# A decoder step on one core: the norms' scales spread by transposes of whole tiles instead of products with the identity

## The chip, the cores and the metric

The kernel runs on one NeuronCore of a Trainium2 chip. Its engines work side by side, each through its own queue in order: TensorE (PE in the profile, its weight loads PEld) multiplies matrices, VectorE (DVE) and ScalarE (ACT) work elementwise, GpSimd (POOL) does small things and issues the DMAs that add into memory, SyncE (SP) issues the other loads and stores. TensorE writes to PSUM, from which DVE and ACT read. The metric is the device time of one execution in microseconds, as the median of several runs; less is better.

## What is computed

One inference step of a small two-layer decoder in float32: 512 new prompt tokens and 8 sequences of 4 new sample tokens, 544 tokens in all, of width 1024. Layer 0 mixes with a short gated convolution, layer 1 with multi-scale retention (4 heads, a state of 256 x 512 for each sequence and head); each is followed by a gated feed-forward block of width 2816.

```python
def rmsnorm(x, g):
    xf = x.astype(jnp.float32)
    y = xf * lax.rsqrt(jnp.mean(xf * xf, axis=-1, keepdims=True) + RMS_EPS)
    return (y * g.astype(jnp.float32)).astype(x.dtype)

def swiglu(x, w_gate, w_up, w_down):
    return (jax.nn.silu(x @ w_gate) * (x @ w_up)) @ w_down

def trunk(x, ...):
    for i in range(DEPTH):
        h = rmsnorm(x, norm_mix[i])
        m, st = short_conv_mixer(h, ...) if i % 2 == 0 else retention_mixer(h, ...)
        x = x + m
        x = x + swiglu(rmsnorm(x, norm_ffn[i]), ffn_w_gate[i], ffn_w_up[i], ffn_w_down[i])
    return rmsnorm(x, final_norm), ...
```

There are thus five norms: the convolution's, the first feed-forward block's, the retention's, the second feed-forward block's and the final one. What the change touches is the per-token factor of each, 1 / sqrt(mean of x squared + eps).

## The kernel before

The activations stand transposed: eight tiles `x[k]` of 128 features (partitions) by 544 tokens (columns), in two halves of HT = 272 tokens. Prompt and sample tokens go through the same matrix products. Each float32 operand is split into a high and a low part (`split`, `split_x`), and a product is three matmuls of 272 columns on these parts (`project`, line 187; `product`, line 386, which does the blocks of a scheme of seven products for two by two). Weights come by SP's queue; for some, the low part is made by ACT writing the negated high part and POOL's queue adding the weights on top with a DMA (`split_adding`, `mixed`, lines 211 and 318).

A norm's gain is applied when the activations are split; its per-token factor is multiplied in only later, behind the products, so that the products need not wait for it. The factor is made by the generator `rms_scale`, whose steps are woven between the matmuls of other products:

1. The squares are summed over the eight tiles into `sqacc` (`square_sum`).
2. Five or six matmuls with one moving column (line 272) take the mean over the 128 partitions, for one tile of 128 tokens each; the result stands as a column of one value per token, in PSUM. Tile 4 is the last 128 tokens (416 to 543), so it overlaps tile 3.
3. `rsqrt` adds eps on DVE and takes the power on POOL, into `rN`, 128 partitions by up to 6 columns.
4. After `rest` more steps of the weave, the scales are spread over all partitions: `spread` (line 252) multiplies the column `rN[:, tt]`, repeated 128 times by a zero step as the stationary operand, with columns of the identity matrix `ident` as the moving operand. Each partition of the output then holds the scales of that tile's tokens along the columns. The tokens are cut where the halves meet: products of 128, 128 and 16 columns fill half 0 (272), of 112, 128 and 32 columns half 1.
5. ACT copies both halves from PSUM into `R` (line 284), which DVE multiplies in later.

`rms_scale` is run by the convolution's stage (its call in line 591), by `ffn` for each of the two layers (`steps = rms_scale(rest=9)`, woven into the first jobs of gate and up), and by `ahead` (retention; its two halves in two banks of PSUM).

The final norm does it by halves, in `final`: `scale(hf)` takes the means (line 923), eps (line 930, DVE) and power (line 931, POOL) for three tiles at columns 0, 128 and 144 of the half, and spreads them by products of 128, 128 and 16 columns. DVE multiplies the outputs with the scales straight from PSUM (`out`, line 949); ACT copies them to `R` for the two tiles that POOL multiplies (line 947). The outputs leave in four stores for each half, by SP's queue and, for the second half's even ones, ACT's. The sums of the second half read `sqacc` and then `sqlast`, the last square, which ACT makes at line 234. Between them `idle(5, ...)` puts five matmuls of ones (line 961).

Elsewhere the kernel transposes with TensorE: the retention's normalized outputs (line 1422) and keys (line 1321) are `nc.tensor.transpose(out, in_, ident)`, where the tile to be turned is the stationary operand and the identity the moving one.

Tile's framework puts the instructions on the engines' queues in program order, with `tc.issue_after` placing a few by hand, and sets the semaphores for each dependence.

Of the kernel before, what the change touches and what calls it, by code (L numbers as in the profile page):

```python
# [12 lines left out]
P = 128  # L13
D = 1024
KT = D // P
SEQ = 512
NB = 8
DS = 4
NS = NB * DS
# [4 lines left out]
HT = T // 2  # L24
# [28 lines left out]
def hybrid_decode_kernel(ctx: ExitStack, tc: tile.TileContext, a: dict, o: dict):  # L53
    nc = tc.nc
# [6 lines left out]
    def nm(s):  # L61
        uid[0] += 1
        return f"{s}_{uid[0]}"
# [3 lines left out]
    kinds, at = ["m"], [0]  # L67
# [5 lines left out]
    def psum():  # L73

        kind = kinds[0][at[0] % len(kinds[0])]
        at[0] += 1
        if kind == "s":
            return [bank(), bank()]
        return ps.tile([P, 2, 512], F32, tag="mm", name=nm("mm"), bufs=2)

    def bank():
        return ps.tile([P, 512], F32, tag="sm", name=nm("sm"), bufs=4)

    def half(pt, hf):
        return pt[hf] if isinstance(pt, list) else pt[:, hf, :]

    def each(fn, pt, *aps):

        if isinstance(pt, list):
            for hf in range(2):  # L90
                fn(pt[hf][:, :HT], *[ap[:, hf, :] for ap in aps])
        else:
            fn(pt[:, :, :HT], *aps)
# [5 lines left out]
    mask_p, where_p, rest = cb[:, :512], cb[:, 512:1024], cb[:, 1024:1312]  # L99
    mask_s, ident, mean_w = rest[:, :NS], rest[:, NS : NS + P], rest[:, NS + P :]  # L100
# [21 lines left out]
    def g_fin(kt):  # L122
        return vec[:, 72 + kt : 73 + kt]
# [10 lines left out]
    rN = resid.tile([P, 6], F32, tag="rN", name="rN")  # L134
# [107 lines left out]
    def rsqrt(out, var, n, eps=None):  # L242

        if eps is None:
            nc.vector.tensor_scalar_add(out, var, EPS)
        else:
            nc.vector.tensor_add(out, var, eps)
        nc.gpsimd.tensor_tensor(out, out, expo[: out.shape[0], :n], op=ALU.pow)

    def spread(out, tt, lo, hi):  # L250

        return nc.tensor.matmul(
            out, rN[:, tt : tt + 1].to_broadcast([P, P]), ident[:, lo:hi], start=True, stop=True, skip_group_check=True
        )

    def rms_scale(sample=False, pt=None, rest=4):

        n = 6 if sample else 5  # L260
        pt = pt or psum()
        ms = half(pt, 0)[:, 496:502]
        cols = [slice(tt * P, (tt + 1) * P) for tt in range(4)] + [slice(T - P, T), slice(SEQ, T)]
        for tt in range(n):
            lhs = sqacc[:, cols[tt]]
            if tt == 5:
                lhs = sqlast[:, :P]
                nc.vector.tensor_copy(
                    lhs.rearrange("p (g c) -> p g c", c=NS),
                    sqacc[:, SEQ:].unsqueeze(1).to_broadcast([P, P // NS, NS]),  # L270
                )
            nc.tensor.matmul(ms[:, tt : tt + 1], lhs, mean_w[:, 0:1], start=True, stop=True)
            if tt < n - 1:
                yield
        rsqrt(rN[:, :n], ms[:, :n], n)
        for _ in range(rest):
            yield

        for tt, hf, at, lo, hi in (
            (0, 0, 0, 0, P), (1, 0, P, 0, P), (2, 0, 2 * P, 0, HT - 2 * P),  # L280
            (2, 1, 0, HT - 2 * P, P), (3, 1, 3 * P - HT, 0, P), (4, 1, SEQ - HT, P - NS, P),
        ):
            spread(half(pt, hf)[:, at : at + hi - lo], tt, lo, hi)
        each(lambda p, r: nc.scalar.activation(r, p, AF.Copy), pt, R)

    def drain(steps):
        for _ in steps:
            pass
# [165 lines left out]
    with ExitStack() as c0:  # L454
# [133 lines left out]

        c, b = temp("c"), temp("b")
        nc.gpsimd.memset(u[:, :, NSLOT : NSLOT + 2], 0.0)  # L590
        steps = rms_scale(rest=5)
        pts = [start()]
        for d, pt in zip((b, c), pts[0]):
            each(lambda p, di: nc.scalar.activation(di, p, AF.Copy), pt, halves(d[:, 0, :]))
# [67 lines left out]
        for i, n in enumerate(PAIRED[0]):  # L662
            if i < 2:
                wh, wl, pt = early[i]
                project(pt, wh, wl, 0, yh, yl, first=False, ks=(KT - 2, KT - 1))
            else:
                wh, wl = load_piece(a["cvout"][n], KT * P)
                pt = psum()
# [4 lines left out]
    def ffn(layer, next_gain, then=None):  # L673
        with ExitStack() as c1:
# [198 lines left out]
            def after(i):  # L873
                if i in behind:
                    later[behind[i]]()

            steps = rms_scale(rest=9)
            run(jobs, (5, 6, 2), after, steps)
            drain(steps)
# [8 lines left out]
    def final(ms, acts, group_weights, fp, tp):  # L888

        ah, al = acts  # L890
        ws = [group_weights(n, ms) for n in range(KT - LATE, KT)]

        sums = {}

        def products(hf):
            c = slice(hf * HT, (hf + 1) * HT)
            for n in range(KT - LATE, KT):
                wh, wl = ws[n - KT + LATE]
                pt = [None, None]
                pt[hf] = bank()  # L900
                project(pt, wh, wl, 0, ah, al, hfs=(hf,))
                nc.vector.tensor_add(x[n][:, c], x[n][:, c], half(pt, hf)[:, :HT])
                square_sum(n, tp, "gu", 4, c=c, add=nc.vector, join=not hf)
                yield

        def gained(hf):

            c = slice(hf * HT, (hf + 1) * HT)
            y = [fp.tile([P, 4, HT], F32, tag="f", name=nm("ya")), tp.tile([P, 4, HT], F32, tag="gu", name=nm("yb"))]
            for kt in range(KT):  # L910
                with tc.issue_after(last_square[0].ins) if hf and kt == KT - 2 else ExitStack():
                    nc.scalar.activation(y[kt // 4][:, kt % 4, :], x[kt][:, c], AF.Copy, scale=g_fin(kt))
            return y

        def scale(hf):
            pt = bank()
            mq = pt[:, 496:499]

            of = (sqacc, sqlast)[: hf + 1]
            for t in of:  # L920
                for i, at in enumerate((0, P, HT - P)):
                    cols = slice(hf * HT + at, hf * HT + at + P)
                    last_sum[hf] = nc.tensor.matmul(
                        mq[:, i : i + 1], t[:, cols], mean_w[:, 0:1], start=t is of[0] and (hf == 0 or i == 0),
                        stop=t is of[-1], skip_group_check=True,
                    )
                if t is not of[-1]:
                    yield
            with tc.issue_after(first_product[0].ins) if hf else ExitStack():
                nc.vector.tensor_scalar_add(rN[:, :3], mq, EPS)  # L930
            powers[hf] = nc.gpsimd.tensor_tensor(rN[:, :3], rN[:, :3], expo[:, :3], op=ALU.pow)
            yield
            for i, (lo, hi) in enumerate(((0, P), (0, P), (3 * P - HT, P))):
                last_spread[0] = spread(pt[:, i * P : i * P + hi - lo], i, lo, hi)
            sums[hf] = pt[:, :HT]

        def copied(hf):

            with tc.issue_after(last_square[0].ins):
                nc.scalar.activation(R[:, hf, :], sums[hf], AF.Copy)  # L940

        def out(hf, y, w):

            yy = y[w // 2][:, w % 2 * 2 : w % 2 * 2 + 2, :]
            if w == 0:
                for i in range(2):
                    nc.gpsimd.tensor_tensor(yy[:, i, :], yy[:, i, :], R[:, hf, :], op=ALU.mult)
            else:
                made = nc.vector.tensor_mul(yy, yy, sums[hf].unsqueeze(1).to_broadcast([P, 2, HT]))
                first_product[0] = first_product[0] or made  # L950
            q = nc.sync if w % 2 or hf == 0 else nc.scalar
            last_store[0] = q.dma_start(o["yT"][hf][:, 2 * w : 2 * w + 2], yy)

        last_sum, last_spread, powers, first_product, last_store = {}, [None], {}, [None], [None]

        def idle(n, ins):

            with tc.issue_after(ins):
                wm = bank()
                for _ in range(n):  # L960
                    last_spread[0] = nc.tensor.matmul(wm[:, :P], ones, ones, start=True, stop=True)

        drain(products(0))
        first, second = scale(0), products(1)
        next(second)
        next(first)
        y0 = gained(0)
        drain(second)
        drain(first)
        out(0, y0, 1)  # L970
        with tc.issue_after(first_product[0].ins):
            copied(0)
        rest = scale(1)
        with tc.issue_after(last_spread[0].ins):
            next(rest)
        next(rest)
        idle(5, last_sum[1].ins)
        y1 = gained(1)
        out(0, y0, 2)
        out(0, y0, 3)  # L980

        with tc.issue_after(last_store[0].ins), tc.issue_after(powers[1].ins):
            out(0, y0, 0)
        drain(rest)
        copied(1)
        for w in range(4):
            out(1, y1, w)
# [782 lines left out]
```

## Time and profile before

| | us |
|---|---|
| median of 3 runs (lowest to highest) | 1404.88 (1404.77 to 1405.04) |
| the profiled execution's own time | 1405.36 |
| its span, first to last instruction | 1403.6 |
| TensorE busy / its weight loads busy | 1390.2 / 1317.3 |
| DVE / ACT / POOL busy | 1132.1 / 822.9 / 219.4 |

All times below are from one profiled execution; a row that begins with a time counts microseconds from the start of the span. In rows of the order of time come start, duration, engine, line, operation, output<-inputs, shapes, and how many instructions were merged into the row; in brackets the idle time of the engine ahead of it and what ended it. For a matmul the first input is the moving operand, the second the stationary one. Rows of the chain of waits have start, duration and what held the chain. Rows of windows have the stretch, its length, each engine's busy time with its number of instructions, the granted clock of TensorE, and the mean share of the 16 DMA engines that was busy with what they moved in GB/s. The durations of matmuls are from their issue to the modelled end, so consecutive ones overlap; the starts tell the pace. The lines of the page and of the other views that matter here stand in the prediction.

### The profile page before, as it was taken

How to read it: one execution, taken by the hardware profiler on the slowest of the kernel's cores; microseconds unless marked ns; L12 is line 12 of the kernel's file. 1: busy time of each engine (PE TensorE's matmuls, PEld its weight loads, DVE VectorE, ACT ScalarE, POOL GpSimd, SP SyncE). 2: the span in 40 equal slices, each digit the busy share in tenths (PEclk: the TensorE clock that was granted, in tenths of full speed). 3: DMA queues.
4: the chain of work that ended last, by engine and by line, in shares of the span. 5: the costliest groups of instructions: out<-in, count | busy, mean ns of one | idle time of the engine just before them, and what ended most of it. 6: DMA issues, size and time to landing. Idle time of an engine off the chain costs nothing.

```text
span 1403.6 us, 26578 instructions
## 1 busy us (share of the span) xinstructions
PE 1390.2 (99%) x10454; PEld 1317.3 (94%) x10454; DVE 1132.1 (81%) x1923; ACT 822.9 (59%) x1286; POOL 219.4 (16%) x255
## 2 busy tenths in 40 slices
PE   9999999999999999999999999999999999999997
PEld 8999999999999999999967877877899999999997
DVE  6987889898989878676867576586799898989884
ACT  7666567667677657666632313224387767677654
POOL 0111011212221213111200000000111212121212
PEclk9999999999999999999999999999999999999999
DMA  6476346777676754677667355465766777777742
GB/s 206 119 169 166 108 106 159 168 173 183 143 188 151 168 120 134 185 199 201 212 212 240 121 209 184 144 235 181 211 143 153 169 176 172 154 184 153 165 106 87
DMA packets 99295, 233.69 MB, mean 166 GB/s; under 512 B 9793, under 2 KB 33489, under 8 KB 98785
## 3 DMA queue, kind: packets, MB, share of 16 engines
q1 hardware_dynamic: 68032, 167.47, 38.4%
q0 software_dynamic: 28688, 56.61, 23.5%
q10 hardware_dynamic: 2448, 7.91, 1.5%
q8 instruction: 82, 1.34, 0.4%
q14 instruction: 45, 0.36, 0.1%
HBM read 191.84 MB, written 28.42 MB: 157 GB/s over the span
## 4 chain that ended last, share of the span: by engine, by line
PE 93%; DVE 2%; issue 2%; DMA 2%; POOL 0%; ACT 0%; SPq 0%; DVEq 0%; POOLq 0%; ACTq 0%
PE sm L386 43%; PE mm L386 16%; PE mm L187 14%; PE sm L187 4%; PE sm L1262 2%; PE sm L1264 2%; PE sm L1263 2%; PE sm L175 2%; PE sm L177 1%; PE sm L176 1%; PE sm L1483 1%; DVE S L1506 1%; PE mm L1270 1%; DMA wl<-in_rtout_dram 1%; PE mm L1422 0%
## 5 line engine op out<-in xcount | busy, mean ns | idle before, releaser
L386 PE MATMUL sm<-oh,wh 128*128 128x272 f32 x856 | 247.8, 289 | 0.5 <-DVE b L447 0.5
L386 PE MATMUL sm<-ol,wh 128*128 128x272 f32 x856 | 246.1, 288 | 0.0
L386 PE MATMUL sm<-oh,wl 128*128 128x272 f32 x856 | 246.1, 287 | 0.0
L202 ACT ACTIVATE h<-w 128x1024 fp32r<-128x1024 f32 (+3 forms) x170 | 136.5, 804 | 106.3 <-PE mm L386 92.9
L203 DVE TENSOR_TENSOR l<-w,h 128x1024 fp32r<-128x1024 f32 (+3 forms) x170 | 153.6, 904 | 28.1 <-ACT h L202 25.3
L315 ACT ACTIVATE wh<-w 128x1024 fp32r<-128x1024 f32 (+1 forms) x134 | 133.7, 998 | 56.7 <-PE sm L386 48.5
L386 PEld LDWEIGHTS sm<-oh,wh 128*128 128x128 f32 x856 | 161.3, 188 | 2.0 <-DVE b L447 0.9
L386 PEld LDWEIGHTS sm<-oh,wl 128*128 128x128 f32 x856 | 161.1, 188 | 0.0
L386 PEld LDWEIGHTS sm<-ol,wh 128*128 128x128 f32 x856 | 160.8, 188 | 0.1
L386 PE MATMUL sm<-parts,wh 128*128 128x272 f32 x736 | 142.5, 288 | 0.0
L202 ACT ACTIVATE wh<-w 128x1024 fp32r<-128x1024 f32 (+3 forms) x76 | 68.0, 898 | 120.3 <-PE mm L187 62.1
L318 POOL DMA_DIRECT2D wl<-in_ffgu_dram x87 | 81.7, 939 | 328.2 <-ACT wl L317 94.2
L386 PE MATMUL mm<-oh,h 128*128 128x272 f32 x396 | 115.5, 292 | 0.0
L386 PEld LDWEIGHTS sm<-parts,wh 128*128 128x128 f32 x736 | 115.5, 188 | 0.0
L386 PE MATMUL mm<-oh,l 128*128 128x272 f32 x396 | 113.5, 287 | 0.0
L386 PE MATMUL mm<-ol,h 128*128 128x272 f32 x396 | 113.3, 286 | 0.0
L316 DVE TENSOR_TENSOR wl<-w,wh 128x512 fp32r<-128x512 f32 (+1 forms) x134 | 87.2, 651 | 26.4 <-ACT wh L315 26.2
L386 PE MATMUL sm<-parts,wl 128*128 128x272 f32 x368 | 106.2, 289 | 0.3 <-DMA wl<-in_rtqk_dram 0.2
L317 ACT ACTIVATE wl<-wh 128x512 fp32r<-128x512 f32 (+1 forms) x173 | 102.8, 594 | 2.0
L203 DVE TENSOR_TENSOR wl<-w,wh 128x1024 fp32r<-128x1024 f32 (+3 forms) x76 | 79.8, 1055 | 13.1 <-ACT wh L202 12.4
L187 PE MATMUL mm<-parts,wh 128*128 128x272 f32 x488 | 82.4, 290 | 1.4 <-ACT wh L202 1.4
L386 PE MATMUL sm<-oh,h 128*128 128x272 f32 x284 | 82.2, 289 | 0.0
(377 smaller groups left out, 3837.7 us busy)
## 6 DMA issues: line engine op xcount, KB each, us to landing
w<-in_ffgu_dram SPq DMA_DIRECT2D x66, 512.0 KB
wl<-in_ffgu_dram POOLq DMA_DIRECT2D x87, 256.0 KB, 5.2
S<-in_rets_dram SPq DMA_DIRECT2D x16, 1024.0 KB
out_rets_dram<-S SPq DMA_DIRECT2D x16, 1024.0 KB
w<-in_ffdn_dram SPq DMA_DIRECT2D x36, 384.0 KB
cb<-in_ffgu_dram SPq DMA_DIRECT2D x22, 512.0 KB
w<-in_cvin_dram SPq DMA_DIRECT2D x21, 512.0 KB
wl<-in_ffdn_dram POOLq DMA_DIRECT2D x48, 192.0 KB, 4.8
```

The costliest lines, as they stand in the source:

```text
L175: nc.tensor.matmul(out, lh, rh, start=start, stop=False, skip_group_check=True)
L187: last_product[0] = nc.tensor.matmul(half(pt, hf)[:, :HT], w[:, c], act[k][:, hf * HT : (hf + 1) * HT], start=(first and k == ks[0] and i ...
L202: h = nc.scalar.activation(dh, src, AF.Copy)
L203: last_low[0] = nc.vector.tensor_sub(dl, src, dh.bitcast(F32))
L315: nc.scalar.activation(wh, w, AF.Copy)
L316: last_mixed[0] = nc.vector.tensor_sub(wl[:, :n], w[:, :n], wh[:, :n].bitcast(F32))
L317: nc.scalar.activation(wl[:, n:], wh[:, n:].bitcast(F32), AF.Copy, scale=-1.0)
L318: nc.gpsimd.dma_start(wl[:, n:], src[:, 1, :] if len(src.shape) == 3 else src[:, n:], accum_op=ALU.add)
L386: last = nc.tensor.matmul(out, w[:, c], b, start=(first and j == 0 and i == 0), stop=(j == len(self.ks) - 1 and i == 2), skip_group_check= ...
L1262: nc.tensor.matmul(out, xh[kt][:, ts_], wh[:, cw], start=(kt == 0), stop=False)
L1263: nc.tensor.matmul(out, xh[kt][:, ts_], wl[:, cw], start=False, stop=False)
L1264: last = nc.tensor.matmul(out, xl[kt][:, ts_], wh[:, cw], start=False, stop=(kt == KT - 1))
```

## The change

`spread` gets a default range (a whole tile) and a flag. Where the range is a whole tile and the flag is on, it calls `nc.tensor.transpose` with the repeated column as the tile to be turned, and the identity as before; the output is the same values in the same place. In `rms_scale` the flag also widens two of the six pieces to whole tiles: tile 2 in half 0 fills columns 256 to 383, of which the first 16 are used, and tile 4 fills columns 144 to 271 of half 1, over what tile 3 has put into 144 to 239 (the same values). The 112 columns of tile 2 that begin half 1 stay a product with the identity. `final` spreads three whole tiles at columns 0, 128 and 144. The convolution's norm passes `turned=False` and keeps its six products.

```diff
-    def spread(out, tt, lo, hi):
+    def spread(out, tt, lo=0, hi=P, turned=True):
 
-        return nc.tensor.matmul(
-            out, rN[:, tt : tt + 1].to_broadcast([P, P]), ident[:, lo:hi], start=True, stop=True, skip_group_check=True
-        )
+        column = rN[:, tt : tt + 1].to_broadcast([P, P])
+        if turned and hi - lo == P:
+            return nc.tensor.transpose(out, column, ident)
+        return nc.tensor.matmul(out, column, ident[:, lo:hi], start=True, stop=True, skip_group_check=True)
 
-    def rms_scale(sample=False, pt=None, rest=4):
+    def rms_scale(sample=False, pt=None, rest=4, turned=True):
...
-        for tt, hf, at, lo, hi in (
-            (0, 0, 0, 0, P), (1, 0, P, 0, P), (2, 0, 2 * P, 0, HT - 2 * P),
-            (2, 1, 0, HT - 2 * P, P), (3, 1, 3 * P - HT, 0, P), (4, 1, SEQ - HT, P - NS, P),
+        whole = (0, P)
+        for tt, hf, at, (lo, hi) in (
+            (0, 0, 0, whole), (1, 0, P, whole), (2, 0, 2 * P, whole if turned else (0, HT - 2 * P)),
+            (2, 1, 0, (HT - 2 * P, P)), (3, 1, 3 * P - HT, whole),
+            (4, 1, HT - P, whole) if turned else (4, 1, SEQ - HT, (P - NS, P)),
         ):
-            spread(half(pt, hf)[:, at : at + hi - lo], tt, lo, hi)
+            spread(half(pt, hf)[:, at : at + hi - lo], tt, lo, hi, turned)
...
-        steps = rms_scale(rest=5)
+        steps = rms_scale(rest=5, turned=False)
...
-            for i, (lo, hi) in enumerate(((0, P), (0, P), (3 * P - HT, P))):
-                last_spread[0] = spread(pt[:, i * P : i * P + hi - lo], i, lo, hi)
+            for i, at in enumerate((0, P, HT - P)):
+                last_spread[0] = spread(pt[:, at : at + P], i)
```

## The prediction

> **What bounds the kernel now.** I read the page first: the busy shares, the clock and the chain that ended last.
>
> ```profile
> span 1403.6 us, 26578 instructions
> ...
> PE 1390.2 (99%) x10454; PEld 1317.3 (94%) x10454; DVE 1132.1 (81%) x1923; ACT 822.9 (59%) x1286; POOL 219.4 (16%) x255
> ...
> PEclk9999999999999999999999999999999999999999
> ...
> PE 93%; DVE 2%; issue 2%; DMA 2%; POOL 0%; ACT 0%; SPq 0%; DVEq 0%; POOLq 0%; ACTq 0%
> ```
>
> TensorE (PE) is busy for 99% of the span at its full clock and holds 93% of the chain. A busy matmul row can hide stalls, since matmuls overlap, so the second view is the table by stage: the two feed-forward stages from their norm's scale spreading on, and the retention stage between them.
>
> ```profile
> 205.56:523.00 317.44, 317.44 (x2531) 316.54 (x2532) 279.38 (x493) 216.33 (x343) 63.41 (x73) 1.00 0.71 160
> 691.00:1028.00 337.00, 335.73 (x2093) 269.53 (x2093) 239.85 (x394) 111.10 (x155) 21.92 (x34) 1.00 0.59 197
> 1049.00:1366.00 317.00, 317.00 (x2531) 316.10 (x2530) 280.35 (x495) 216.00 (x343) 63.40 (x73) 1.00 0.72 160
> ```
>
> The columns behind the length are PE, PE's weight loads, DVE, ACT, POOL, then the clock and the DMA share. In both feed-forward stages PE has no idle time at all, and 317.44 us for 2531 matmuls is 0.125 us for each: a matmul taken out there is worth its spacing. In the retention stage PE idles for 1.3 us of 337. The third view is that of the line which spreads the scales.
>
> ```profile
> L252 PEld LDWEIGHTS mm<-cb,rN x36: 186/190/193, 33.9 to 1050.4; 128*128 128x128 f32 x36
> L252 PE MATMUL mm<-cb,rN x36: 182/275/377, 34.0 to 1050.4; 128*128 128x128 f32 x18, 128*128 128x16 f32 x6, 128*128 128x112 f32 x6, 128*128 128x32 f32 x6
> L252 PEld LDWEIGHTS sm<-cb,rN x24: 185/190/192, 561.2 to 1394.9; 128*128 128x128 f32 x24
> L252 PE MATMUL sm<-cb,rN x24: 182/275/376, 561.3 to 1395.0; 128*128 128x128 f32 x14, 128*128 128x16 f32 x6, 128*128 128x112 f32 x2, 128*128 128x32 f32 x2
> ```
>
> The code issues 30 products there (four norms of 6, two halves of the final norm of 3), and the trace has 60 records: each float32 product is two passes, each with its own weight load.
>
> **The change part by part.** In the built program the changed kernel has the same instructions in the same order, with the same waits, on DVE, ACT, POOL and SP, and on PE everywhere but at five places. So it moves no DMA and adds no wait. Three norms (both feed-forward norms, the retention norm) go from 6 products to 5 transposes and 1 product; the two halves of the final norm from 3 products to 3 transposes; the convolution's 6 stay.
>
> The price of what is there, from the order of time of the weight loads, at the three norms:
>
> ```profile
> 205.56 1.41 PEld L252 LDWEIGHTS mm<-cb,rN 128*128 128x128 f32 x12 [0.22 <-POOL rN L248]
> 206.89 0.19 PEld L386 LDWEIGHTS sm<-oh,wh 128*128 128x128 f32 x1
> ...
> 561.17 1.43 PEld L252 LDWEIGHTS sm<-cb,rN 128*128 128x128 f32 x12
> 562.52 0.19 PEld L187 LDWEIGHTS sm<-parts,wh 128*128 128x128 f32 x1
> ...
> 1049.12 1.43 PEld L252 LDWEIGHTS mm<-cb,rN 128*128 128x128 f32 x12
> 1050.47 0.19 PEld L386 LDWEIGHTS sm<-oh,wh 128*128 128x128 f32 x1
> ```
>
> From the first load of the spreading to the next load of the stream are 1.33, 1.35 and 1.35 us, for 12 records: 0.1125 us each. That the narrow ones (16 and 32 columns) are in this mean says that the load, not the width, sets the pace; so it costs nothing that the change widens two of them to whole tiles.
>
> The price of a transpose is in the trace too, since the retention stage transposes whole float32 tiles with the same identity as moving operand:
>
> ```profile
> 741.41 0.47 PEld L1422 LDWEIGHTS mm<-cb,yn 128*128 128x128 f32 x4
> 741.85 0.19 PEld L175 LDWEIGHTS sm<-mid,qkhl 128*128 128x128 f32 x1
> ...
> L1422 PE MATMUL mm<-cb,yn 128*128 128x128 f32 x64 | 9.9, 277 | 0.5 <-DVE gate L1428 0.3
> ```
>
> One record for each (4 calls, 4 records), and (741.85 - 741.41) / 4 = 0.11 us from one to the next, with ordinary matmuls right ahead and behind. The one thing that this row doesn't have is a stationary operand that is one column repeated by a zero step; the products of L252 load the same operand in the 190 ns that other float32 loads take, so I give it no price. Between 0.11 (this spacing) and 0.277 (this row's duration, if nothing overlapped) I take 0.11, since the row is the same instruction.
>
> Each of the three norms then takes 5 x 0.11 + 2 x 0.1125 = 0.775 us. Saved: 0.555 + 0.575 + 0.575 = 1.705 us, on PE where it has no idle time. ACT waits for these products to copy the scales (4.7 us in all over five copies by the same view); it waits less, which is worth nothing, for PE does not wait for the scales in these stages.
>
> The two halves of the final norm lie in the tail, where other things end last.
>
> ```profile
> 1386.73 0.45 DVE sqacc L236
> ...
> 1387.32 0.80 PE sm L923 x6
> ...
> 1390.94 0.76 PEld L252 LDWEIGHTS sm<-cb,rN 128*128 128x128 f32 x6
> 1391.62 0.75 PEld L923 LDWEIGHTS sm<-cb,sqacc 128*128 128x128 f32 x6
> 1392.29 0.75 PEld L923 LDWEIGHTS sm<-cb,sqlast 128*128 128x128 f32 x6
> 1392.96 0.19 PEld L961 LDWEIGHTS sm<-ones 128*128 128x128 f32 x1
> ...
> 1391.73 0.43 ACT L234 ACTIVATE sqlast<-x 128x272 f32<-128x272 f32 x1 [0.18 <-DVE x L902]
> ```
>
> The first half's 6 records take 0.68 us (1390.94 to 1391.62); three transposes take 0.33, so 0.35 is saved on PE. But of the sums behind them, the second six read the square that ACT finishes at 1391.73 + 0.43 = 1392.16, from a residual sum that no spreading feeds. After DVE's last addition for the first half (1386.73 + 0.45 = 1387.18) PE's sums began at 1387.32, 0.14 later; so these could begin at about 1392.30 and begin now at about 1392.3. The cover is gone at once: the square is late next, PE idles for the 0.35 us, and I take 0 (bounds 0 and 0.35).
>
> ```profile
> 1394.38 0.85 PE sm L252 x6
> ...
> 1394.30 2.91 POOL L947 TENSOR_TENSOR ya<-ya,R 128x272 f32<-128x272 f32 x4
> ...
> 1397.67 0.42 ACTq L952 DMA_DIRECT2D out_yT_dram<-yb  x1
> ...
> 1395.50:1396.00 0.50, 0.00 (x0) 0.00 (x0) 0.32 (x1) 0.15 (x1) 0.50 (x2) 1.00 1.00 370
> 1397.50:1398.00 0.50, 0.00 (x0) 0.00 (x0) 0.17 (x1) 0.00 (x0) 0.00 (x0) 1.00 1.03 400
> 1398.00:1398.50 0.50, 0.00 (x0) 0.00 (x0) 0.00 (x0) 0.00 (x0) 0.00 (x0) 1.00 0.91 318
> ```
>
> The second half's products end some 3 x 0.1125 = 0.34 us earlier, and DVE's last products with them. Yet the last store of ACT's queue (1397.67) stands behind the store of POOL's products, which run without a break from 1394.30 to 1397.21 from POOL's own power on, and the DMA engines are full from 1395.5 on (share 1.00, 1.03) but for a hole of 0.09 x 0.5 = 0.045 us. I take that hole, 0.05 us (bounds 0 and 0.34).
>
> Sum: 1.705 + 0 + 0.05 = 1.75 us. The profiled execution's span goes from 1403.6 to 1401.85 and its own time from 1405.36 to 1403.61; the median of the runs shown (1404.88) lies 0.48 under the profiled one, so the median goes to **1403.1**.
>
> **The rivals.** *Given back at the next wait.* PE waits for a landing at two places behind the first two norms.
>
> ```profile
> PE mm L187 <- DMA wl<-in_rtout_dram: 0.3, 1, 0.3
> ...
> PE sm L386 <- DMA wl<-in_rtqk_dram: 0.2, 1, 0.2
> ...
> 616.25 4.12 PE sm L386 x31
> 620.37 0.03 POOLq L318
> ...
> 622.42 5.00 DMA wl<-in_rtqk_dram
> ...
> 1020.71 7.03 DMA wl<-in_rtout_dram
> ```
>
> If these loads don't come earlier with PE, what the first two norms saved (0.555 + 0.575) is lost there, and 1.75 - 1.13 = 0.62 us stay: 1404.3. Against it: the chain behind the first landing leads back through POOL's issue to PE's own matmuls, so the load moves with PE.
>
> *Slower: transposes that don't overlap in these places.* If the repeated column made each wait for the one before, it would cost its duration, 0.277 us. Each norm: 5 x 0.277 + 0.225 = 1.61, that is 0.28 + 0.26 + 0.26 = 0.80 us more; the first half of the final norm 0.83 against 0.68, 0.15 more on the chain; the second 0.83 against 0.85. Together 0.95 more: 1405.8. It decides from 0.224 us (two passes of 0.1125) for a transpose on, and to be slower by 0.2% each of the 18 would need 0.224 + 2.81 / 18 = 0.38 us. The row at 741.41 speaks against it.
> The Trainium skill ("TensorE: Matmul & The Clock Gate", Part 4) gives about 390 ns for a transpose in isolation (bf16) and 275 ns in a kernel; an estimate by 390 would be 18 x (0.390 - 0.224) = 3.0 us slower, 1407.9. The durations of 277 ns agree with its second figure, but the spacing of 0.11 is what the stream pays.
>
> *Slower: a landing slips.* The two landings above took 5.00 and 7.03 us; if PE's new phase made both 2.03 us later, 4.06 - 1.75 = 2.3 us would be lost: 1407.2. It decides from 1.75 us of added waiting. Only two waits of at most 0.3 us in 1.4 ms speak for it.
>
> *Faster: a transpose at a quarter of the product.* At 0.056 us each norm takes 0.505 us and the three save 2.52: 1402.3 with the tail. Against it: the sums of L923 move a single column, and their 12 records from 1391.62 to 1392.96 are still 0.112 us apart, so a load of 128 columns alone holds the spacing.
> The same page ("TensorE: Matmul & The Clock Gate", Terms) calls the transpose mode four times faster for FP32, which would be this rival; the rows show half (0.11 for 0.225), and the measurement decides.
>
> **How the numbers follow.** The forecast 0.74 (own range 1402.5, with all of the tail's 0.69 saved, to 1403.9); given back 0.10; no overlap 0.03; a slip 0.05; a quarter 0.04; something that the profile doesn't show 0.04, to either side. About 0.2%, 2.81 us, is what a measurement of this kernel can tell from no change, so "same" reaches from 1402.07 to 1407.69 and holds nearly all of the first three, most of the slip and of the quarter: 0.85. Faster than that 0.09 (the quarter with all of the tail, tails of the forecast, half of the unseen), slower 0.06 (a slip past its price, the other half). The range from 1402.2 (the quarter) to 1404.7 (the give-back with the runs' scatter of 0.3) leaves out 0.16.
>
> **What would show it.** Right: each of the three norms shows 7 records within about 0.78 us from its first weight load to the next load of the stream; PE's share of 317 us stays full behind them; the time between the last norm's spreading (1049.12) and the first half's (1390.94) shrinks by about 0.57; ahead of the second sums of the final norm PE idles by 0.3; the last stores go out as they do now, with the landing the same distance behind POOL's power. Wrong: transposes 0.2 us apart or more; waits at the landings of rtqk or rtout grown by over 0.5 us; an end that follows the second half's spreading by 0.3 us less than now.

## The result and the profile after

The changed kernel takes 1402.84 us in the median against 1405.01 for the kernel before in the same session, 2.2 us less. The ratio is 0.9984 with a 95% interval from 0.9977 to 0.9990, that is 1.4 to 3.2 us less: clear of no change, with the median inside the 0.2% that the prediction called "same". One of the 22 executions of the changed kernel took 2728.96 us, in the slow state, for a reason that the record does not show; the ratio leaves it out, and without it the median is 1402.75. A second set of runs of the same kernel, described below, gave 1402.98 against 1405.11, ratio 0.9986 (0.9977 to 0.9995).

The head of the page and the chain of the profiled execution after (its own time 1401.96):

```profile
span 1400.2 us, 26536 instructions
...
PE 1388.3 (99%) x10433; PEld 1315.7 (94%) x10433; DVE 1132.3 (81%) x1923; ACT 822.8 (59%) x1286; POOL 219.4 (16%) x255
...
PE 92%; DVE 4%; DMA 2%; issue 1%; ACT 1%; POOL 0%; DVEq 0%; SPq 0%; POOLq 0%; ACTq 0%
```

10454 matmul records became 10433: 21 fewer, five at each of three norms and three in each half of the final one. The other engines' counts are the same, and by line and tile names all other instructions stand in the same order in both traces. What bounds the kernel has not changed.

The weight loads in order of time at the three norms (start, duration, engine, line; L254 is the transpose, L255 the product, the last row of each group the next load of the stream):

```profile
204.47 0.30 PEld L254 LDWEIGHTS mm<-cb,rN 128*128 128x128 f32 x3 [0.22 <-POOL rN L248]
204.75 0.30 PEld L255 LDWEIGHTS mm<-cb,rN 128*128 128x128 f32 x2
204.95 0.25 PEld L254 LDWEIGHTS mm<-cb,rN 128*128 128x128 f32 x2
205.18 0.19 PEld L389 LDWEIGHTS sm<-oh,wh 128*128 128x128 f32 x1
...
559.32 0.36 PEld L254 LDWEIGHTS sm<-cb,rN 128*128 128x128 f32 x3
560.08 0.55 PEld L187 LDWEIGHTS sm<-parts,wh 128*128 128x128 f32 x4
...
1046.39 0.36 PEld L254 LDWEIGHTS mm<-cb,rN 128*128 128x128 f32 x3
1047.16 0.19 PEld L389 LDWEIGHTS sm<-oh,wh 128*128 128x128 f32 x1
```

From the first load to the stream's next are 0.71, 0.76 and 0.77 us, where they were 1.33, 1.35 and 1.35. To three digits, from the same loads, the savings are 0.634, 0.592 and 0.590 us.

The tail, in order of time: the first half's transposes and the sums behind them, the square that the second sums read, POOL's products and ACT's last store:

```profile
1387.62 0.36 PEld L254 LDWEIGHTS sm<-cb,rN 128*128 128x128 f32 x3
1387.96 0.75 PEld L926 LDWEIGHTS sm<-cb,sqacc 128*128 128x128 f32 x6
1388.89 0.74 PEld L926 LDWEIGHTS sm<-cb,sqlast 128*128 128x128 f32 x6 [0.18 <-ACT sqlast L234]
...
1388.41 0.43 ACT L234 ACTIVATE sqlast<-x 128x272 f32<-128x272 f32 x1 [0.19 <-DVE x L905]
...
1390.90 2.91 POOL L950 TENSOR_TENSOR ya<-ya,R 128x272 f32<-128x272 f32 x4
...
1394.28 0.42 ACTq L955 DMA_DIRECT2D out_yT_dram<-yb  x1
```

The sums on `sqacc` start 0.34 us behind the first transpose instead of 0.68, and then TensorE waits for the square, which it did not before: 1387.96 to 1388.89 for six loads that take 0.67. All but 0.06 us of the 0.35 saved in the first half is eaten there: the loads of the second sums, those on `sqlast`, begin 4.91 us after the final norm's first sums (1383.98), where it was 4.97 (1387.32 to 1392.29). POOL's products again run 2.91 us without a break and ACT's last store follows them. From the end of POOL's products to the end of the span it is 6.38 us in both kernels. From the first sums to the end it is 16.21 us; it was 16.27 (from 1387.32 to 1403.59). The 0.06 us of the second sums is thus the whole gain of the tail, and the second half adds nothing to it.

These five places make 0.634 + 0.592 + 0.590 + 0.063 = 1.88 us. The two profiled spans differ by 3.4. The rest, 1.5 us, is at places that the change does not touch, and the experiments had to say whether it belongs to the change.

### The profile page after: what moved, and what is told of

It reads as the page before. It is cut to its first block, busy times and chain, and to the rows that moved or that the text cites. A ratio compares the mean times of both kernels' runs of the same rounds, so it can differ in the third digit from the quotient of the medians.

```text
span 1400.2 us, 26536 instructions
## 1 busy us (share of the span) xinstructions
PE 1388.3 (99%) x10433; PEld 1315.7 (94%) x10433; DVE 1132.3 (81%) x1923; ACT 822.8 (59%) x1286; POOL 219.4 (16%) x255
## 3 DMA queue, kind: packets, MB, share of 16 engines
q8 instruction: 81, 1.33, 0.4%
## 4 chain that ended last, share of the span: by engine, by line
PE 92%; DVE 4%; DMA 2%; issue 1%; ACT 1%; POOL 0%; DVEq 0%; SPq 0%; POOLq 0%; ACTq 0%
PE sm L389 44%; PE mm L389 16%; PE mm L187 13%; PE sm L187 4%; PE sm L1265 2%; PE sm L1267 2%; PE sm L1266 2%; PE sm L175 2%; PE sm L177 1%; PE sm L176 1%; PE sm L1486 1%; DVE S L1509 1%; PE mm L1273 1%; DMA rot<-km 0%; PE mm L1425 0%
```

## The experiments

To see where time goes, each profile was cut at the spreadings, from the end of one (the stream's next weight load) to the first load of the next. The spreadings themselves are left out. Column by column, in us: from the start to the convolution's spreading, then the convolution stage, the first feed-forward block, the retention stage and the second feed-forward block; then the tail, from the first sums of the final norm to the end. The last two columns overlap by 3.6 us, since the second feed-forward column runs to the final norm's first spreading.

| run | start | conv | ffn 0 | retention | ffn 1 | tail |
|---|---|---|---|---|---|---|
| before | 33.92 | 170.28 | 354.28 | 486.60 | 340.46 | 16.27 |
| changed | 33.27 | 169.85 | 354.15 | 486.31 | 340.47 | 16.21 |
| changed again | 33.80 | 169.57 | 354.14 | 486.52 | 340.42 | 16.22 |
| final as products | 34.37 | 170.14 | 354.19 | 486.82 | 340.46 | 16.30 |
| only the final turned | 32.92 | 170.23 | 354.20 | 487.46 | 340.42 | 16.20 |
| products nine times | 32.65 | 169.88 | 354.55 | 488.42 | 340.42 | 16.30 |
| transposes nine times | 33.29 | 170.36 | 354.35 | 486.79 | 340.43 | 16.20 |
| tail twice | 33.34 | 170.24 | 354.19 | 486.22 | 340.49 | 16.31 |
| second half eight times | 33.16 | 170.21 | 354.14 | 487.50 | 340.42 | 18.20 |
| conv turned too | 33.21 | 175.50 | 354.19 | 488.15 | 340.42 | 16.18 |
| six transposes | 32.92 | 173.80 | 354.20 | 488.33 | 340.46 | 16.19 |
| conv, one turned | 33.76 | 176.53 | 354.14 | 486.98 | 340.40 | 16.21 |
| conv, four turned | 34.02 | 170.28 | 354.14 | 487.11 | 340.40 | 16.20 |
| together | 33.73 | 170.53 | 354.16 | 487.93 | 340.41 | 16.20 |

The feed-forward columns hold to 0.15 us wherever nothing was repeated. The start scatters by 1.7 us and the retention stage by 2.2, whatever the kernel.

### The final norm back to products

```diff
-            for i, at in enumerate((0, P, HT - P)):
-                last_spread[0] = spread(pt[:, at : at + P], i)
+            for i, (lo, hi) in enumerate(((0, P), (0, P), (3 * P - HT, P))):
+                last_spread[0] = spread(pt[:, i * P : i * P + hi - lo], i, lo, hi, False)
```

> The final norm goes back to its three products per half; the three other norms keep their transposes. Theory (all of the gain is the 15 records saved at three norms, on a TensorE that has no idle time behind them; the final norm's records are covered by the last square and by the store train): as fast as the changed kernel within 0.3 us, about 2 us under before; in the trace the three norms take 0.70, 0.76 and 0.76 us from the first weight load to the next load of the stream, and from the first sums of the final norm to the end of the span it is 16.27 us as before, against 16.2 in the changed kernel. Rival (the final norm's six saved records count too): 0.6 to 0.7 us slower than the changed kernel, about 1.5 under before, the tail 0.6 longer than the changed kernel's.

Measured: 1403.40 against 1404.88, ratio 0.9987 (0.9978 to 0.9996), 0.6 to 3.1 us less. The median lies at the rival's 1.5 us, but with this interval it cannot tell the theory (2 us) from it. The trace can: the three norms at 0.70, 0.76 and 0.76 us, and a tail of 16.30 us, 0.09 more than the changed kernel's and not 0.6.

### Only the final norm turned

```diff
-            steps = rms_scale(rest=9)
+            steps = rms_scale(rest=9, turned=False)
...
-        steps = rms_scale(True, [bank(), bank()])
+        steps = rms_scale(True, [bank(), bank()], turned=False)
```

> Only the final norm's spreading is transposed; the three other norms keep their products. Theory: 0 to 0.1 us under before, which the runs can't tell from no change; TensorE idles about 0.25 us more ahead of the second sums of the final norm, and the tail is 16.2 us. Rival (the tail counts): 0.6 to 0.7 us under before. A second rival (much of the 2.2 us is scatter of the loads at the start and of two landings, not the change): the three norms at 1.35 us each, and still a start or waits that differ from before by 0.5 to 1 us.

Measured: 1404.84 against 1404.88, ratio 1.0000 (0.9992 to 1.0009), a tail of 16.20. The final norm's six saved records are worth 0.07 to 0.1 us. Its start is 32.92 us, 1 us shorter than before's and shorter than the changed kernel's, though three norms have their products here: a short start is not the change's doing.

### Every spreading product nine times, and every transpose nine times

In the kernel before:

```diff
-            spread(half(pt, hf)[:, at : at + hi - lo], tt, lo, hi)
+            for _ in range(times):
+                spread(half(pt, hf)[:, at : at + hi - lo], tt, lo, hi)
```

with `times` 9 at three norms and 1 at the convolution's. In the changed kernel:

```diff
-            spread(half(pt, hf)[:, at : at + hi - lo], tt, lo, hi, turned)
+            for _ in range(9 if turned else 1):
+                spread(half(pt, hf)[:, at : at + hi - lo], tt, lo, hi, turned)
```

> The kernel before, with each spreading product of the two feed-forward norms and the retention norm issued nine times in a row (the same values into the same place). Theory: 8 x 12 x 0.1125 = 10.8 us more at each of three norms, 32.4 us more than before in the time. Rival (the spreading hides behind waits): clearly less.

> The changed kernel with the same repetition: five transposes and one product, each nine times, at three norms. Theory: a transpose of the repeated column costs 0.11 us and the product 0.225, so 8 x 0.77 = 6.2 us more at each norm, 18.5 more than the changed kernel and 16.3 over before; 16.1 under the nine products, nine times the 1.8 us of the single change. Rival (transposes of the same column that follow each other stall at 0.277 us): 8 x 1.61 = 12.9 us at each norm, 38.6 more than the changed kernel. Rival (a quarter of the product, 0.056 us): 12.1 us more than the changed kernel.

Measured: the products 1437.82 against 1405.19, 32.6 us more where 32.4 were expected. The transposes 1422.79, 17.6 more than before where 16.3 were expected. In place, the repetition of the transposes at the retention's norm shows as (start, duration, engine, line, how many):

```profile
566.21 2.98 PEld L254 LDWEIGHTS sm<-cb,rN 128*128 128x128 f32 x27
569.16 2.09 PEld L255 LDWEIGHTS sm<-cb,rN 128*128 128x128 f32 x18
571.15 2.00 PEld L254 LDWEIGHTS sm<-cb,rN 128*128 128x128 f32 x18
573.12 0.43 PEld L187 LDWEIGHTS sm<-parts,wh 128*128 128x128 f32 x3
```

27 transposes in a row, nine of each of three repeated columns, take 2.95 us, 0.109 each; the 18 passes of the product 1.99, 0.111 each. From 0.76 us the place grows to 6.91, 0.77 for each repetition, as expected; the products' place grows from 1.35 to 12.05, 1.34 for each. Neither rival holds: not 0.277 us, not 0.056. The three places of the transposes hold 16.6 us more than before; the measured 17.6 has an interval of 15.9 to 20.1, so that the 1.0 us between them is not told from scatter.

### The final norm's transposes twice

```diff
             for i, at in enumerate((0, P, HT - P)):
-                last_spread[0] = spread(pt[:, at : at + P], i)
+                for _ in range(2):
+                    last_spread[0] = spread(pt[:, at : at + P], i)
```

> The changed kernel with each transpose of the final norm issued twice, 0.33 us more of TensorE's work in each half. Theory: the tail (first sums of the final norm to the end of the span) stays at 16.2 to 16.3 us: in the first half the square sets the second sums, in the second half the store train. Rival: the tail grows by 0.33 to 0.66 us.

Measured: a tail of 16.31 us. 0.66 us of added work on TensorE cost 0.1: the second sums now follow the transposes without an idle stretch.

### The second half's transposes eight times

The same loop with `range(8 if hf else 1)`.

> The changed kernel with each transpose of the final norm's second half issued eight times, 21 x 0.11 = 2.3 us more ahead of its outputs. Theory: the scales then come too late for POOL, which has about 0.4 us of slack behind its own products (1391.95 against 1392.37 in the changed kernel), so the tail grows by about 1.9 us, to 18.1. Rival (stores alone set the end): the tail grows by less than 1 us. Rival (no slack): 2.3 us.

Measured: a tail of 18.20 us. In order of time, the transposes, ACT's copy of the scales, POOL's last two products and ACT's first store:

```profile
1392.37 2.59 PEld L254 LDWEIGHTS sm<-cb,rN 128*128 128x128 f32 x24 [0.22 <-POOL rN L934]
...
1395.24 0.40 ACT L944 ACTIVATE R<-sm 128x272 f32<-128x272 f32 x1 [3.90 <-PE sm L254]
1395.71 1.48 POOL L951 TENSOR_TENSOR ya<-ya,R 128x272 f32<-128x272 f32 x2 [1.96 <-ACT R L944]
1397.22 0.34 ACTq L956 DMA_DIRECT2D out_yT_dram<-ya  x1
```

POOL now idles 1.96 us for the scales, and the end moves by 2.0. So in the changed kernel the second half's spreading has a slack of some 0.3 us and then counts in full. In the kernel before, POOL's four products already ran without a break, so it did not wait for the scales there either: what the transposes saved became this slack.

The run also tells whether the full DMA engines set the end. While POOL waits they run dry (the last two columns are their busy share and GB/s):

```profile
1395.50:1396.00 0.50, 0.00 (x0) 0.00 (x0) 0.33 (x1) 0.14 (x1) 0.29 (x1) 1.00 0.07 22
1396.50:1397.00 0.50, 0.00 (x0) 0.00 (x0) 0.50 (x2) 0.00 (x0) 0.50 (x1) 1.00 0.03 13
```

Yet the end still comes 6.39 us after POOL's last product (1395.71 + 1.48 = 1397.19 to 1403.58), as it does with full engines. The backlog of stores does not set it; POOL's products and the stores behind them do.

### The convolution's norm turned too

```diff
-        steps = rms_scale(rest=5, turned=False)
+        steps = rms_scale(rest=5)
```

> The convolution's norm is transposed too. Theory (TensorE's stream is the path there as well): its spreading goes from 1.35 to 0.76 us, and the kernel is 0.6 us faster than the changed one, 2.4 to 2.8 under before. Rival (given back: behind the convolution's norm TensorE waits at about 109 and 114 us for DVE's and ACT's work, which doesn't come earlier): the 0.6 us are lost by 115 us, and the kernel is as fast as the changed one.

Measured: 1408.77 against 1404.88, ratio 1.0026 (1.0016 to 1.0037): 3.9 us slower than before, and 6 slower than the changed kernel in its own session. Both expectations were wrong. The spreading did go to 0.76 us, but the convolution stage grew from 170 to 175.5 us. The wait lies in it, by the view of who waited for whom (engine and line, waited for: us, times, longest):

```profile
PE sm L389 <- DMA wl<-in_cvin_dram: 2.8, 1, 2.8
PE sm L389 <- DVE c L450: 0.8, 1, 0.8
```

In the same stretch (40 to 130 us) the changed kernel has only one wait, 0.4 us for DVE. What differs is the order. By line and tile names, 275 of the 10394 matmul records that spread no scales stand in another place than in the changed kernel's trace, with 42 instructions of DVE's, 39 of ACT's and 2 of POOL's (the DMA that adds a low part from `in_cvin` has changed places with the one into `yl`). So the order of the instructions is not that of the program alone, as the part on the kernel before had it: the framework plans it, and since the edit exchanges one kind of instruction for another, the plan depends on the kind. That it goes by a cost which it gives to each kind is likely, but no run shows it.

### Six whole transposes at four norms

The scales are laid 16 columns further on in each half, so that no piece is cut, and ACT copies from there:

```diff
+        off = HT - 2 * P
+        for tt, hf, at in ((0, 0, off), (1, 0, off + P), (2, 0, off + 2 * P), (2, 1, 0), (3, 1, P), (4, 1, off + HT - P)):
+            spread(half(pt, hf)[:, at : at + P], tt)
...
+            nc.scalar.activation(R, pt[:, :, off : off + HT], AF.Copy)
...
-        steps = rms_scale(rest=5, turned=False)
+        steps = rms_scale(rest=5)
```

> All four norms spread by six whole transposes and no product: the halves lie 16 columns further on in PSUM, so that tile 2 fits whole into the second half too, and ACT copies from there. Theory: six records at 0.11 us, 0.67 us for each norm against 0.76, so 0.1 us less at each of three norms and 0.7 less at the convolution's: 1.0 us under the changed kernel, 2.8 to 3.2 under before. Rival (the convolution's share given back, as above): 0.3 under the changed kernel.

Measured: 1407.55 against 1404.88, ratio 1.0018 (1.0009 to 1.0027), 2.7 us slower than before; a miss as well. The three norms take 0.60, 0.66 and 0.66 us as expected. The convolution stage takes 173.80: but for ten matmuls, two of DVE's and five of ACT's instructions it has the same other order, and TensorE waits 2.9 us for the same landing.

### One piece of the convolution's norm turned

From here on each of the convolution norm's six pieces has a flag of its own:

```diff
+        flags = (True,) * 6 if turned else (True, False, False, False, False, False)
...
-            spread(half(pt, hf)[:, at : at + hi - lo], tt, lo, hi, turned)
+            spread(half(pt, hf)[:, at : at + hi - lo], tt, lo, hi, flag)
```

> The changed kernel, with one of the convolution norm's six products (the first tile) as a transpose. As built, this puts the instructions of the convolution's products into the other order that the kernel with the whole convolution norm transposed had. Theory (that kernel lost its 5 us to the order, which the planner makes from its costs, not to the transposes): the stretch from the convolution's spreading to the next norm's grows from 171.2 to 171.7 us to about 177, and the kernel is 5 to 6 us slower than the changed one. Rival (the transposes themselves disturb the convolution's stage): one of five transposes costs a fifth, 1 us.

Measured: 1408.12 against 1405.11, ratio 1.0025 (1.0015 to 1.0035); 5.1 us slower than the changed kernel beside it. The convolution stage takes 176.53 us (177.8 with the spreading, as the expectation counts it). By line and tile names its order is that of the kernel with the whole convolution norm turned, instruction for instruction. One transposed piece costs as much as five:

```profile
33.76 0.13 PEld L254 LDWEIGHTS mm<-cb,rN 128*128 128x128 f32 x1
33.87 1.20 PEld L255 LDWEIGHTS mm<-cb,rN 128*128 128x128 f32 x10
...
PE sm L390 <- DMA wl<-in_cvin_dram: 3.0, 1, 3.0
```

The place itself is quick (11 loads instead of 12); the 3.0 us wait for a low part comes later, at 76 us.

The three kernels in the other order wait 2.8, 2.9 and 3.0 us there, but their convolution stages differ by up to 2.7 us. Behind the wait, TensorE's granted clock falls to 0.50 in this kernel for some 6.8 us and in the one with the whole norm turned for some 3.4 us; in the one with six transposes it stays at 1.00. The same two microseconds, here and with six transposes:

```profile
82.00:84.00 2.00, 2.00 (x11) 2.00 (x11) 0.00 (x0) 0.52 (x2) 0.00 (x0) 0.50 0.79 258
82.00:84.00 2.00, 2.00 (x18) 2.00 (x17) 1.03 (x4) 0.63 (x1) 0.00 (x0) 1.00 0.15 57
```

An estimate from these rows, 6.8 us at 11 matmuls instead of 18, is 2.6 us lost. So most of what the order costs is this wait, and a slower clock behind it can add to it; why the clock fell in two of three profiles after waits of nearly the same length is open.

### Four pieces of the convolution's norm turned

Flags `(True, True, True, False, False, True)`, for which the order is that of the changed kernel but for eight of TensorE's matmuls that stand swapped.

> Four of the convolution norm's pieces as transposes (the first, the second and the third in the first half, the last in the second half), two as products: a mix for which the built order stays that of the changed kernel but for eight matmuls of one stretch. Theory: the convolution's spreading goes from 1.35 to about 0.9 us (4 x 0.11 + 4 x 0.1125), its stage stays at 171 to 172 us, and the kernel is 0.4 us faster than the changed one. Rival (the transposes disturb the stage): 3 to 5 us slower than the changed one.

Measured: 1403.56 against 1405.11, ratio 0.9989 (0.9980 to 0.9998). The convolution's spreading takes 0.89 us, its stage 170.28 (171.2 with the spreading): four transposes in place and no 5 us. So the transposes themselves do not slow the stage, and the other order is what the slow kernels have in common; the six products in that order were not run. The 0.46 us that the place saves do not show in the time, which is 0.6 over the changed kernel's beside it instead of 0.4 under, both with intervals of 2.5 us: that part of the expectation is not borne out.

### Both together

> The same four transposes in the convolution's norm, and six whole transposes with the halves 16 columns on in the other three. Theory: 0.45 us less at the convolution's norm and 0.10 at each of three others than in the changed kernel, 0.75 in all, 2.6 under before. Rival (the loads' scatter covers it): not told from the changed kernel.

Measured: 1404.11 against 1405.11, ratio 0.9993 (0.9984 to 1.0002); a miss: it is not told from before, and lies 1.1 us over the changed kernel beside it. In place all is as expected:

```profile
205.15 0.63 PEld L254 LDWEIGHTS mm<-cb,rN 128*128 128x128 f32 x6 [0.22 <-POOL rN L248]
205.75 0.19 PEld L400 LDWEIGHTS sm<-oh,wh 128*128 128x128 f32 x1
...
PE sm L400 <- ACT g L459: 0.9, 1, 0.9
PE mm L400 <- ACT b L459: 0.4, 1, 0.4
```

0.60 us for six transposes, a saving of 0.77 us in all four places over the changed kernel. The profiled run loses it in the convolution stage (170.53) and in the retention stage (487.93), by waits such as these two, at 1038 and 109 us. Whether the earlier arrival lengthens them or they scatter is open: the run with the second half eight times, whose instructions up to the tail are the changed kernel's, has 0.9 us at the wait for `g` too, and a stage of 487.50. No version here is shown to beat the changed kernel.

### The changed kernel once more

> The changed kernel once more, beside these. Theory: the same three norms (0.70, 0.76 and 0.76 us) and tail (16.2 us); the start up to the convolution's spreading (33.3 in the first profile) and the retention stage differ by up to 1 us, since other runs of the same instructions scatter by as much, so its span is nearer to 1.9 us under before than to the 3.4 of the first profile. Rival (the change itself made the start and the retention stage shorter): a start of 33.3 and a retention stage of 487.1 us again.

Measured: 1402.98 against 1405.11, ratio 0.9986 (0.9977 to 0.9995). The norms take 0.70, 0.76 and 0.77 us, the start 33.80 instead of 33.27, and the retention stage 486.52 instead of 486.31: for the start the theory holds, for the retention stage this run is near the first. Its span, 1400.6, is 3.0 us under the one profile of before, still nearer to the 3.4 than to 1.9, so on the span the expectation failed. Of the 3.0, 0.12 is the start, 0.7 the convolution stage (169.57, the shortest of all runs, with the same instructions as in before), 0.14 the first feed-forward block.

## Why the prediction was right

The forecast was 1403.1 and the median is 1402.84. Step by step:

**TensorE without idle time behind the norms.** Held. Both feed-forward columns of the table stay within 0.15 us while their spreadings shrink by 0.6: what was taken out in place came out of the sum. Behind the retention's norm the stage scatters by more than the 0.59 us saved, so for that norm alone the table does not show it. The nine-fold products cost 32.6 us for 32.1 in place at the three norms, so time put there counts in full.

**The price of a record.** 0.1125 us for a pass and 0.11 for a transpose, predicted from other rows, measured 0.111 and 0.109. That a zero step in the stationary operand costs nothing was assumed and is shown by the nine-fold transposes. The sum of three norms was mis-sized by 6%: 1.705 predicted, 1.816 measured. The transpose behind the product's second pass loads 0.097 us after it, and at the first norm, where TensorE had idled for POOL, the first three loads take 0.28 us and not 0.33.

**The tail.** 0.05 predicted, 0.06 measured, against 0.69 of work counted as saved. The size is right by luck, for it comes from the other half. The prediction put the first half at 0, since it let the second sums begin 0.14 us after the square, as the first sums do after DVE's last addition; behind ACT's square their loads began after 0.05 (1388.41 + 0.43 = 1388.84 to 1388.89), and the 0.06 was gained there. The cover itself, the wait for the square, is the one named: 0.26 us from when the first six loads are through to the next one (1387.96 + 0.67 = 1388.63 to 1388.89). The prediction's 0.05 was to come from the second half, out of a hole in the DMA engines' work. That half gave nothing: the end follows its first weight load by 9.21 us before (1394.38 to 1403.59) and 9.22 after (1390.97 to 1400.19). What covers it is POOL's chain, which the prediction named too, and not the full DMA engines: with these nearly empty in the eight-fold run, the end came no sooner behind POOL's last product. That run, 2.3 us of added work for 2.0 us of end, puts the slack there at 0.3 us.

**The rivals.** *Given back* did not happen: the waits for `in_rtqk` and `in_rtout` are gone from the changed kernel's list for matmuls, which is, in full:

```profile
PE sm L488 <- DVE expo L108: 1.1, 1, 1.1
PE sm L389 <- DVE b L450: 0.4, 1, 0.4
PE sm L1425 <- DVE yn L1401: 0.3, 2, 0.2
PE sm L389 <- ACT oh L202: 0.2, 1, 0.2
PE sm L926 <- DVE sqacc L236: 0.2, 1, 0.2
PE sm L187 <- DVE wl L203: 0.2, 1, 0.2
```

In the weight loads' own list `in_rtout` is gone too (0.5 us before), and `in_rtqk` stands with 0.3 us instead of 0.4: it has not grown. That the matmuls' wait for `in_rtout` (0.3 us before) is gone is worth up to 0.3 us on top, but the run with only the final norm turned waits 0.5 us there, and the one with nine-fold products 1.1 us for `in_rtg`: these landings come and go. *A slip* of this kind is thus real, at 0.2 to 1.1 us and not the 4 that the rival priced. *No overlap* and *a quarter* are refuted by the 0.109 us of 27 in a row. The Trainium skill ("TensorE: Matmul & The Clock Gate", Terms) has the transpose mode four times faster for FP32; here a product is two passes of 0.111 us and a transpose one of 0.109, a factor of two.

**What decided it without being a term.** The prediction rested on the same order everywhere else, which the traces of the two kernels have. The convolution runs show the weight of that step: where the order did change, the convolution stage grew by 4 to 7 us, at least twice the whole gain.

What stays open is the difference between 1.88 us in the five places and the 2.2 of the medians. The interval of 1.4 to 3.2 covers it, and the start and the retention stage scatter by more.

## What to carry to other kernels

In the full stream of this kernel the price of an operation was the spacing of its starts, not its duration: 0.109 against 0.277 us, and the rows of the same operation elsewhere in the kernel gave it to within 2%. A saving counts where the engine has no idle time behind it; in a tail, look for what else is due at the same moment, for there a saving only becomes slack (0.3 us here). A term of the right size can still stand at the wrong place, so check where a gain arises and not only how large it is. Where a framework plans the order, compare the order of the instructions before judging an edit: exchanging one product for a cheaper transpose cost 5 us along with instructions that stood elsewhere, while four such exchanges that kept the order cost nothing that could be measured.

## What the runs showed of the hardware

The same instructions take from 32.65 to 34.37 us to the convolution's spreading, and 486.2 to 488.4 us in the retention stage. This scatter is as large as the effect under study. At the start it goes with a landing: the one of `x` in the chain took 4.40 us where the start was 32.92 (only the final norm turned) and 6.15 where it was 34.37 (the final norm as products). The two feed-forward stages, in which TensorE has no idle time, repeat to 0.15 us.

A weight load for a transpose of float32 has a duration of 0.13 to 0.15 us against 0.19 for a product's. In a full stream that changes nothing (0.109 against 0.111 us from load to load), but behind an idle stretch the second transpose's load came 0.055 us after the first, where a product's came 0.108 after.

Behind a wait of 2.8 to 3.0 us of TensorE in the convolution stage, the granted clock fell to 0.50 for 3.4 and 6.8 us in two of three profiles, with 11 matmuls in 2 us instead of 18.
